# A two-layer encoder on one core: the gate's rows through DRAM and a broadcast load in place of TensorE transposes

## The chip, the core and the metric

The kernel runs on one core of one Trainium2 chip. The metric is device time in microseconds (us), the median of several executions. Engines are named as the profile names them: PE is TensorE (matrix products; PEld are its weight loads), DVE is VectorE, ACT is ScalarE, POOL is GpSimd, SP is SyncE, which here only issues DMAs. Each engine takes its instructions in the order in which they stand; a DMA that an engine issues stands in that engine's queue too.

## The reference, cut to what matters

Two layers, each a mixer and a gated convolutional FFN, on x of 512 tokens by 1024 channels in float32. Every one of the four sub-layers is wrapped in the same way:

```python
m = silu(c) @ w + b                       # c: 1 x 1024, w: 1024 x 3072
shift, scale, gate = split(m, 3)
h = x * (1.0 + scale) + shift
x = layer_norm(ALPHA * x + (1.0 + gate) * f(h), g, b)
```

So each sub-layer needs one row of 1024 gates, the same for all tokens. f is a spatial-gating and pooling mixer (sub-layer 0), a Conformer convolution module (2), and a conv-FFN of inner width 2816 (1 and 3).

## The kernel before, in words

Tokens are held as four tiles x_94 to x_97 of 128 tokens (partitions) by 1024 channels. A float32 product is made of three passes: each operand is split into a rounded part and the remainder (whi and wlo for weights, hhi and hlo for h, ahi and alo for activations), ACT casting the first, DVE subtracting for the second, and PE does high by high, high by low, low by high (`mm3`). Weights come in tiles of 128 by 1024 (512 KB) through SP's queue into four buffers w, and are split into seven buffers each of whi and wlo. PSUM has eight banks `ps`.

The modulations are dot products on DVE: rows of `in_ada` are loaded, multiplied with silu(c) on all partitions and summed, so that channel 128 c + p of a modulation stands in column c of partition p of `mods[i]` (128 by 24; the gate is columns 16 to 23). `gate_column` (line 199) makes the tile gcol, 128 by 8, of (1 + gate) / ALPHA. The accumulations `accumulate` (line 233) and `take` (line 378) multiply a PSUM tile, tokens on partitions, with the gate, so they want the row of 1024 gates on every partition: the tile gate, 128 by 1024, one buffer. `gate_bcast` (line 204) makes it: eight times it gives PE one column of gcol, repeated 128 times, as the weights, and the identity as the moving operand, which puts the column's 128 values into 128 columns of PSUM on all partitions; ACT copies the two filled banks into gate.

This happens four times: `gate_bcast(g0)` in the mixer of layer 0 (line 729, its column made at line 636), in each `ffn` at tile i = 10 (line 466), and in the Conformer module at tile i = 4 (line 919).

The order of the work is fixed in two ways. In the mixer of layer 0 (`in_order`, `pool_order` on) every instruction keeps the place in which it is written. Elsewhere only pinned ones do; the tile framework's scheduler, which plans with a model of the times, places the others. So an edit also moves instructions that it doesn't name. In the FFN of layer 0 (`ffn` with `side0`, `ahead0`) DVE does the dot products of three modulations beside the convolutions, POOL builds diagonal matrices whi and wlo from the identity and the taps (`diagonal`), and SP's queue holds weight loads, loads of in_ada, and stores (keephi, keeplo) of those diagonals and of split weights for layer 1, all in one line. `to_next` (line 395) ends a sub-layer: for each token tile it finishes the output product, takes the statistics on DVE (`take`), centres x (`centre`), transposes x on PE and makes the next h.

Of the kernel before, what the change touches and what calls it, by code (L numbers as in the profile page):

```python
# [7 lines left out]
F32 = mybir.dt.float32  # L8
# [4 lines left out]
P = 128  # L13
D = 1024
# [76 lines left out]
def body(ctx, tc, a):  # L91
# [8 lines left out]
    def psum():  # L100
        return pp.tile([P, 512], F32, name="ps")

    def tmp(n=512, dtype=F32):
        return tp.tile([P, TW], dtype, name="t")[:, 0:n]
# [4 lines left out]
    T, V, A, Q = (_Engine(e, pin, in_order) for e in (nc.tensor, nc.vector, nc.scalar, nc.sync))  # L109
    G = _Engine(nc.gpsimd, pin, pool_order)  # L110

    def behind(ins, other):

        if other is not None:
            tc.add_manual_dep(ins.ins, other.ins.name, ORDER, reason="issue order")
        return ins
# [13 lines left out]
    ident = const.tile([P, P], F32, name="ident")  # L130
# [4 lines left out]
    def col(name, i, n=1):  # L135
        at, _ = _COLS[name]
        return cols[:, at + i : at + i + n]


    def load(src):  # L140
        w = wp.tile([P, 1024], F32, name="w", bufs=4)
        Q.dma_start(w, src)
        return w
# [4 lines left out]
    def parts(w, after=None, eng=None, low_after=None, at=slice(0, 1024)):  # L148
        hi = wp.tile([P, 1024], F32R, name="whi", bufs=7)[:, at]
        lo = wp.tile([P, 1024], F32R, name="wlo", bufs=7)[:, at]  # L150
        w = w[:, at]
        if eng is None:
            behind(A.copy(hi, w), after)
        else:
            eng.tensor_copy(hi, w)
        behind(V.tensor_tensor(lo, w, hi.bitcast(F32), ALU.subtract), low_after)
        return hi, lo
# [5 lines left out]
    dp = ctx.enter_context(tc.tile_pool(name="dram", bufs=1, space=bass.MemoryType.DRAM))  # L163
# [32 lines left out]
    def ada_bias(i, j, n=1):  # L196
        V.tensor_tensor(mods[i][:, j : j + n], mods[i][:, j : j + n], col("ada_b", 24 * i + j, n), ALU.add)

    def gate_column(i):
        g = sm.tile([P, 8], F32, name="gcol")  # L200
        V.tensor_scalar(g, mods[i][:, 16:24], 1.0, 1.0 / ALPHA, ALU.add, ALU.mult)
        return g

    def gate_bcast(g):

        out = hp.tile([P, D], F32, name="gate", bufs=1)
        for h in range(2):
            ps = psum()
            for k in range(4):
                one = g[:, 4 * h + k : 4 * h + k + 1]  # L210
                T.transpose(ps[:, k * P : (k + 1) * P], one.broadcast_to([P, P]), ident)
            A.copy(out[:, h * 512 : (h + 1) * 512], ps)
        return out

    def affine(i, ln):
# [33 lines left out]
    def new_h():  # L249
        return (hp.tile([P, KD, S], F32R, name="hhi", bufs=1), hp.tile([P, KD, S], F32R, name="hlo", bufs=1))  # L250
# [61 lines left out]
    def split_act(ap_, t):  # L312
        return act_lo(act_hi(ap_, t))
# [12 lines left out]
    def out_half(acts, wsrc, d, gate, before=None, side=None):  # L326

        pss = [psum() for _ in range(ST)]
        nk = 2 * len(wsrc)
        for kp in range(nk // 2):  # L330
            w = ready(wsrc[kp])
            if side:
                side()
            for k in (2 * kp, 2 * kp + 1):
                if before:
                    before(k)
                for s in range(ST):
                    out_one(pss[s], acts, w, k, s, nk, before is not None)
        for s in range(ST):
            accumulate(s, d, pss[s], gate, G)  # L340
# [89 lines left out]
    def proj_tiles(h, srcs, after=None):  # L430

        out = []
        for s_ in srcs:
            w = tuple(v.rearrange("p (k m) -> p k m", k=KD) for v in ready(s_, after))
            ps = psum()
            for k in range(KD):
                mm3(ps, sl(w, slice(None), k), sl(h, slice(None), k), k == 0, k == KD - 1)
            out.append(ps)
        return out

    def conv3(l, f, ps):
        at = l * 132
        acc = tmp()
        A.activation(acc, ps, AF.Identity, bias=col("ffn_dw_b", l * 44 + f), scale=col("ffn_dw", at + 44 + f))
        V.scalar_tensor_tensor(acc[:, 1:S], ps[:, 0 : S - 1], col("ffn_dw", at + f), acc[:, 1:S], ALU.mult, ALU.add)
        V.scalar_tensor_tensor(acc[:, 0 : S - 1], ps[:, 1:S], col("ffn_dw", at + 88 + f), acc[:, 0 : S - 1], ALU.mult, ALU.add)
        return acc

    def ffn(ap_, l, h, ps4, last, mod_i, side, side_out=None):

        def pair(i, pg, pv):
            g = conv3(l, i, pg)
            v = conv3(l, NF + i, pv)
            gl = tmp()
            A.activation(gl, g, AF.Gelu_apprx_tanh)
            V.tensor_tensor(gl, gl, v, ALU.mult)
            return split_act(ap_, gl)

        w = a["ffn_up"]
        acts = []  # L460
        for i in range(NF):
            pg, pv = ps4[2 * i : 2 * i + 2] if i < 2 else proj_tiles(h, [w[l, 2 * i], w[l, 2 * i + 1]], last[0] if i < 5 else None)
            acts.append(pair(i, pg, pv))
            side(i)
            if i == 10:
                gate = gate_bcast(gate_column(mod_i))
            if i == SPLIT - 1:
                for d in range(2):
                    out_half(acts, [a["ffn_downA"][l, d, kp] for kp in range(SPLIT // 2)], d, gate, side=side_out)
                acts = []  # L470
        out_half(acts, [a["ffn_downB"][l, 0, kp] for kp in range((NF - SPLIT) // 2)], 0, gate, side=side_out)
        return acts, gate


    h = new_h()
    in_order.on = pool_order.on = True
    with tc.tile_pool(name="l0", bufs=1) as l0, tc.tile_pool(name="l0a", bufs=8) as ap_:
# [71 lines left out]
        def mod_dot(*js):  # L549
            for j in js:  # L550
                ada_dot(1, j, place(j))
# [50 lines left out]
        for hd in range(4):  # L602
            ps = psum()
# [5 lines left out]
        def sgu_gate(hd):  # L609
            ps, t = mixed[hd], us[hd]  # L610
            n_ = ps.rearrange("p (n q) -> p n q", n=ST)
            V.scalar_tensor_tensor(n_, n_, col("sgu_g", hd), bsb[:, hd : hd + 1, :].broadcast_to([P, ST, P]), ALU.mult, ALU.add)
            V.tensor_tensor(t, ps, t, ALU.mult)
            return act_hi(ap_, t)
# [12 lines left out]
        p = [sgu_gate(0), sgu_gate(1)]  # L627
# [4 lines left out]
        p = [sgu_gate(2), sgu_gate(3)]  # L632
        gate_dot(22, 23)
        fetch(x[1], a["x"][1])
        ada_bias(0, 16, 8)
        g0 = gate_column(0)
        mod_dot(0, 1)
        acts[2], acts[3] = (act_lo(q) for q in p)
        zr = []
# [77 lines left out]
        out0(5)  # L717
        acts[5], acts[4] = act_lo(p1), act_lo(p0)
        wl[2] = parts(wl[2])
        up = [load(a["ffn_up"][0, j]) for j in range(2)]  # L720
        mod_dot(14, 15)
        wl[3] = parts(wl[3])
# [3 lines left out]
        up[1] = parts(up[1])  # L726
        ada_bias(1, 0, 16)
        ga_be = affine(1, 0)
        gate = gate_bcast(g0)
        for s in range(ST):  # L730
            accumulate(s, 0, pss[s], gate, G)
        in_order.on = pool_order.on = False
        h, ps4, last = to_next(order, wl, gate, ga_be, [*up, a["ffn_up"][0, 2], a["ffn_up"][0, 3]])
# [36 lines left out]
    def side0(i):  # L770
        deferred(0, i)
        if i == 2:
            A.copy(taps_hi, taps)
            V.tensor_tensor(taps_lo, taps, taps_hi.bitcast(F32), ALU.subtract)
        if i >= 9 and todo_d:
            diagonal(*todo_d.pop(0))
        if i in (13, 15, 17):
            ahead0()
        for _ in range(3 if i >= 2 else 0):
            if todo:  # L780
                m, j = todo.pop(0)
                ada_tile(m, j, first)
                if j == 23:
                    ada_bias(m, *((16, 8) if m == 1 else (0, 24)))

    with tc.tile_pool(name="taps", bufs=1) as tp_, tc.tile_pool(name="f0", bufs=12) as ap_:
        taps_hi = tp_.tile([P, TAPS * KD], F32R, name="taphi")
        taps_lo = tp_.tile([P, TAPS * KD], F32R, name="taplo")
        acts, gate = ffn(ap_, 0, h, ps4, last, 1, side0, ahead0)
        h, ps4, last = to_next(acts, [a["ffn_downB"][0, 1, kp] for kp in range((NF - SPLIT) // 2)], gate, affine(2, 1), [a["cv_in"][j] for j in range(4)])  # L790


    with tc.tile_pool(name="l1", bufs=1) as l1, tc.tile_pool(name="l1a", bufs=25) as ap_:
# [119 lines left out]
        for i in range(KD):  # L913
            if i < 2:
                pa, pg = ps4[2 * i], ps4[2 * i + 1]
            else:
                pa, pg = proj_tiles(h, nxt)
                if i == 4:
                    gate = gate_bcast(gate_column(2))
                if i + 1 < KD:  # L920
                    nxt = [recall(("cv_in", j)) for j in (2 * i + 2, 2 * i + 3)]
                advance(now[0], V_TAPS)
            glu(i, pa, pg)
            if i:
                advance(now[1], G_TAPS)
            advance(todo_d, D_TAPS)
# [129 lines left out]
        h, ps4, last = to_next(acts, wo[1], gate, affine(3, 2), [a["ffn_up"][1, j] for j in range(4)], 2)  # L1056
# [9 lines left out]
    with tc.tile_pool(name="f1", bufs=12) as ap_:  # L1066
        acts, gate = ffn(ap_, 1, h, ps4, last, 3, side1)
# [105 lines left out]
```

## Time and profile before

| what | value |
|---|---|
| median of 3 runs | 1080.02 us (1079.01 to 1080.77) |
| the profiled execution | 1076.26 us |
| its span, first to last instruction | 1074.5 us |
| granted TensorE clock, mean over the span | 0.997 |
| PE busy | 1051.1 us, 98% of the span |
| DVE, ACT, POOL busy | 787.1, 462.2, 266.0 us |
| DMA | 214.23 MB, mean 199 GB/s |

The profiled execution is one run, 3.76 us below the median of the three timed ones; 1.76 us of it lie around the span. Of a row of a timeline the first number is the start in us from the span's start, the second what it took; a bracket at the end gives how long the engine was idle before it and what released it. Matmuls overlap in such rows (a matmul is shown with 0.39 us, and the next starts 0.23 us later), so PE's cost is read from starts.

### The profile page before, as it was taken

The numbers are of one execution on the slowest core, as the hardware profiler recorded it, in microseconds if no ns is written. First come the engines' busy times: TensorE is split into PE (matmuls) and PEld (weight loads), VectorE is DVE, ScalarE is ACT, GpSimd is POOL, SyncE is SP. The second block draws the span as 40 slices with busy tenths as digits, with TensorE's granted clock in tenths as the row PEclk, the third lists the DMA queues.
The fourth block names the chain that finished last, engine by engine and source line by source line (L and its number), as shares of the span: only waits on it lengthen the run. The fifth ranks groups of instructions, "written<-read, shape, count | busy, mean of one in ns | idle before, by whom it ended". The sixth has DMA issues, their size and how long they took to land.

```text
span 1074.5 us, 13947 instructions
## 1 busy us (share of the span) xinstructions
PE 1051.1 (98%) x5157; PEld 882.4 (82%) x5157; DVE 787.1 (73%) x1173; ACT 462.2 (43%) x676; POOL 266.0 (25%) x309
## 2 busy tenths in 40 slices
PE   6999999999999999999999999899999999999997
PEld 5888798888888887888988987798888888888886
DVE  6788879979966889956399999777676333656537
ACT  4544464433742444633666743564444212434300
POOL 0000200057026940001199995200000022000011
PEclk9999999999999999999999999999999999999999
DMA  9979418777998898971555471233332233323302
GB/s 353 408 264 369 169 42 280 268 266 258 384 413 333 335 331 306 337 294 59 222 210 191 157 260 50 99 121 116 117 118 85 92 98 99 98 98 99 98 1 78
DMA packets 61555, 214.23 MB, mean 199 GB/s; under 512 B 6960, under 2 KB 6960, under 8 KB 61488
## 3 DMA queue, kind: packets, MB, share of 16 engines
q1 hardware_dynamic: 59184, 209.16, 54.3%
q10 hardware_dynamic: 2304, 4.20, 1.6%
q8 instruction: 40, 0.66, 0.2%
q14 instruction: 27, 0.22, 0.1%
HBM read 182.13 MB, written 31.20 MB: 199 GB/s over the span
## 4 chain that ended last, share of the span: by engine, by line
PE 89%; DVE 5%; DMA 4%; POOL 2%; ACT 0%; issue 0%; SPq 0%; DVEq 0%; POOLq 0%
PE ps L85 89%; DMA w<-in_ffn_up 1%; DVE t L85 1%; DVE wlo L85 1%; DMA w<-in_cv_out 1%; POOL whi L85 1%; DMA w<-in_ab_in 1%; DVE ps L85 1%; DVE st L85 1%; DVE w L85 1%; ACT whi L85 0%; POOL wlo L85 0%; DMA whi<-keephi_cv_out 0%; POOL x L85 0%; DVE x L85 0%
## 5 line engine op out<-in xcount | busy, mean ns | idle before, releaser
L85 PE MATMUL ps<-hhi,whi 128*128 128x512 f32 (+1 forms) x960 | 353.1, 369 | 0.3 <-ACT whi L85 0.3
L85 PE MATMUL ps<-hhi,wlo 128*128 128x512 f32 (+1 forms) x960 | 352.8, 368 | 0.5 <-DVE wlo L85 0.5
L85 PE MATMUL ps<-hlo,whi 128*128 128x512 f32 (+1 forms) x960 | 352.9, 368 | 0.0
L85 DVE TENSOR_TENSOR wlo<-w,whi 128x1024 fp32r<-128x1024 f32 x176 | 219.1, 1253 | 167.1 <-ACT whi L85 163.8
L85 ACT CAST whi<-w 128x1024 fp32r<-128x1024 f32 x175 | 183.1, 1051 | 304.4 <-PE ps L85 180.6
L85 PEld LDWEIGHTS ps<-hhi,wlo 128*128 128x128 f32 x960 | 181.0, 188 | 31.1 <-DVE wlo L85 1.0
L85 PEld LDWEIGHTS ps<-hlo,whi 128*128 128x128 f32 x960 | 181.0, 189 | 29.8
L85 PEld LDWEIGHTS ps<-hhi,whi 128*128 128x128 f32 x960 | 180.5, 189 | 30.3 <-ACT whi L85 0.7
L85 POOL TENSOR_TENSOR x<-x,t 128x512 f32<-128x512 f32 x32 | 48.4, 1540 | 537.7 <-DVE t L85 537.7
L85 PE MATMUL ps<-whi,ahi 128*128 128x512 f32 (+1 forms) x426 | 167.8, 394 | 0.0
L85 PE MATMUL ps<-whi,alo 128*128 128x512 f32 (+1 forms) x426 | 166.3, 390 | 0.0
L85 PE MATMUL ps<-wlo,ahi 128*128 128x512 f32 (+1 forms) x426 | 166.3, 390 | 0.0
L85 DVE SCALAR_TENSOR_TENSOR t<-ps,cols,t 128x511 f32<-128x511 f32 x176 | 130.2, 745 | 5.9 <-ACT t L85 4.3
L85 POOL TENSOR_TENSOR a<-a 128x512 f32<-128x512 f32 (+1 forms) x99 | 104.7, 1094 | 23.6 <-ACT a L85 23.1
L85 ACT ACTIVATE t<-ps,cols 128x512 f32<-128x512 f32 (+1 forms) x108 | 78.1, 740 | 42.7 <-PE ps L85 41.2
L85 PEld LDWEIGHTS ps<-wlo,ahi 128*128 128x128 f32 x426 | 80.2, 188 | 18.7 <-issue 0.5
L85 PEld LDWEIGHTS ps<-whi,ahi 128*128 128x128 f32 x426 | 80.1, 188 | 18.6 <-issue 0.5
L85 PEld LDWEIGHTS ps<-whi,alo 128*128 128x128 f32 x426 | 80.1, 188 | 18.5
L85 DVE CUSTOM_DVE_ANT_0 w<-w,cb 128x1024 f32<-128x1024 f32 x56 | 69.6, 1251 | 9.2 <-DMA w<-in_ada 9.1
L85 ACT ACTIVATE a<-a,cols 128x512 f32<-128x512 f32 (+1 forms) x105 | 62.9, 634 | 26.5 <-POOL a L85 25.4
L85 DVE SCALAR_TENSOR_TENSOR ps<-a,cols,ps 128x512 f32<-128x512 f32 (+1 forms) x122 | 72.2, 661 | 0.0
L85 POOL TENSOR_SCALAR whi<-ident,taphi 128x128 fp32r<-128x128 f32 x62 | 47.3, 781 | 85.0 <-DMA w<-in_ffn_up 75.1
(105 smaller groups left out, 980.6 us busy)
## 6 DMA issues: line engine op xcount, KB each, us to landing
w<-in_ffn_up SPq DMA_DIRECT2D x88, 512.0 KB, 4.2
w<-in_ada SPq DMA_DIRECT2D x56, 512.0 KB, 4.6
x<-in_ada SPq DMA_DIRECT2D x24, 512.0 KB, 7.7
w<-in_ffn_downA SPq DMA_DIRECT2D x24, 512.0 KB, 4.2
w<-in_ffn_downB SPq DMA_DIRECT2D x20, 512.0 KB, 4.4
w<-in_cv_in SPq DMA_DIRECT2D x16, 512.0 KB, 6.9
keephi_cv_in<-whi SPq DMA_DIRECT2D x12, 512.0 KB, 6.3
keeplo_cv_in<-wlo SPq DMA_DIRECT2D x12, 512.0 KB, 6.3
```

What stands on the lines that cost most here:

```text
L85: ins = getattr(self.engine, name)(*args, **kw)
```

## The change

The transposes, their two PSUM banks and ACT's two copies go. In their place each gate column is written to a DRAM row of 1024 floats as soon as it is made, by a DMA that POOL issues: element by element, 128 partitions by 8 values of 4 bytes. The tile gate is then filled by one DMA on SP's queue that reads the row for all 128 partitions (512 KB moved). In the mixer of layer 0 the load is written into SP's line ahead of the loads of the FFN's first weights; elsewhere the scheduler sets its place.

```diff
-    def gate_bcast(g):
+    gate_rows = {}
+
+    def gate_out(i):
+
+        gate_rows[i] = dp.tile([1, D], F32, name=f"gate{i}")
+        G.dma_start(gate_rows[i].rearrange("o (c p) -> p (o c)", p=P), gate_column(i))
+
+    def gate_bcast(i):
 
         out = hp.tile([P, D], F32, name="gate", bufs=1)
-        for h in range(2):
-            ps = psum()
-            for k in range(4):
-                one = g[:, 4 * h + k : 4 * h + k + 1]
-                T.transpose(ps[:, k * P : (k + 1) * P], one.broadcast_to([P, P]), ident)
-            A.copy(out[:, h * 512 : (h + 1) * 512], ps)
+        Q.dma_start(out, gate_rows[i].partition_broadcast(P))
         return out
...
             if i == 10:
-                gate = gate_bcast(gate_column(mod_i))
+                gate = gate_bcast(mod_i)
...
         ada_bias(0, 16, 8)
-        g0 = gate_column(0)
+        gate_out(0)
...
         wl[2] = parts(wl[2])
+        gate = gate_bcast(0)
         up = [load(a["ffn_up"][0, j]) for j in range(2)]
...
         ga_be = affine(1, 0)
-        gate = gate_bcast(g0)
...
                 if j == 23:
                     ada_bias(m, *((16, 8) if m == 1 else (0, 24)))
+                    gate_out(m)
...
                 if i == 4:
-                    gate = gate_bcast(gate_column(2))
+                    gate = gate_bcast(2)
```

The scheduler moves other instructions with it. Three places of the lines follow, before and of the change (in names, a number such as 94 in x_94 is a buffer's own; ISA is DVE's dot product).

First, DVE at the end of the mixer of layer 0, from the accumulations with the gate (t<-ps,gate) to the first token tile's statistics. Before:

```order
L85 TENSOR_TENSOR t<-ps,gate 128x512 x4
L85 BN_STATS st<-x_94 128x6
L85 TENSOR_TENSOR wlo<-w,whi 128x1024
L85 BN_STATS st<-x_95 128x6
L85 BN_STATS st<-x_96 128x6
L85 BN_STATS st<-x_97 128x6
L85 TENSOR_TENSOR t<-ps,gate 128x512
L85 TENSOR_TENSOR x_94<-x_94,t 128x512
L85 BN_STATS st<-x_94 128x6
L85 BN_AGGR mv<-st 128x2
```

Of the change:

```order
L85 TENSOR_TENSOR t<-ps,gate 128x512 x4
L85 TENSOR_TENSOR wlo<-w,whi 128x1024
L85 BN_STATS st<-x_94 128x6
L85 BN_STATS st<-x_95 128x6
L85 TENSOR_TENSOR t<-ps,gate 128x512
L85 BN_STATS st<-x_96 128x6
L85 TENSOR_TENSOR x_94<-x_94,t 128x512
L85 BN_STATS st<-x_97 128x6
L85 BN_STATS st<-x_94 128x6
L85 BN_AGGR mv<-st 128x2
```

The weight's remainder wlo now stands ahead of all four first statistics, so one more of them lies between it and the first tile's BN_AGGR.

Second, DVE in the FFN of layer 0 at the middle of its down-projection, where the third gate column is made. Before:

```order
L85 TENSOR_SCALAR ga<-mod_92 128x8
L85 TENSOR_SCALAR gcol<-mod_92 128x8
L85 TENSOR_TENSOR be<-ga,cols 128x8
L85 TENSOR_TENSOR be<-be,mod_92 128x8
L85 TENSOR_TENSOR ga<-ga,cols 128x8
L85 TENSOR_TENSOR wlo<-w,whi 128x1024
L85 TENSOR_TENSOR t<-ps,gate 128x512 x4
L85 TENSOR_TENSOR wlo<-w,whi 128x1024 x2
```

Of the change:

```order
L85 TENSOR_SCALAR gcol<-mod_92 128x8
L85 TENSOR_SCALAR ga<-mod_92 128x8
L85 TENSOR_TENSOR t<-ps,gate 128x512
L85 TENSOR_TENSOR be<-ga,cols 128x8
L85 TENSOR_TENSOR t<-ps,gate 128x512
L85 TENSOR_TENSOR be<-be,mod_92 128x8
L85 TENSOR_TENSOR ga<-ga,cols 128x8
L85 TENSOR_TENSOR wlo<-w,whi 128x1024
L85 TENSOR_TENSOR t<-ps,gate 128x512 x2
L85 TENSOR_TENSOR wlo<-w,whi 128x1024 x2
```

The first wlo, of the weights that PE multiplies with next, has gone behind two of the accumulations. On POOL the write of the row stands at the same place, ahead of the adds x<-x,t that these accumulations feed, and the diagonal that stood there goes behind two of the adds:

```order
L85 DMA gate_3119<-gcol 128x8x1
L85 TENSOR_TENSOR x_94<-x_94,t 128x512
L85 TENSOR_TENSOR x_95<-x_95,t 128x512
L85 TENSOR_SCALAR whi<-ident,taphi 128x128 x8
L85 TENSOR_TENSOR x_96<-x_96,t 128x512
L85 TENSOR_TENSOR x_97<-x_97,t 128x512
L85 TENSOR_SCALAR wlo<-ident,taplo 128x128 x8
```

Before, five of those whi and no DMA stood ahead of the add to x_94.

Third, SP's line later in the same FFN, where two weight loads for PE stand beside the store of a split weight for layer 1 (the numbers are tiles'). Before:

```order
L85 DMA w<-in_ada 128x1024 x3
L85 DMA keephi_cv_out_1_3673<-whi 128x1024
L85 DMA keeplo_cv_out_1_3674<-wlo 128x1024
L85 DMA w<-in_ffn_up 128x1024 x2
L85 DMA w<-in_ada 128x1024 x3
```

Of the change:

```order
L85 DMA w<-in_ada 128x1024 x3
L85 DMA keephi_cv_out_1_3659<-whi 128x1024
L85 DMA w<-in_ffn_up 128x1024
L85 DMA keeplo_cv_out_1_3660<-wlo 128x1024
L85 DMA w<-in_ffn_up 128x1024
L85 DMA w<-in_ada 128x1024 x3
```

The first weight load no longer stands behind the store that waits for DVE's wlo.

## Rows read from the trace of the kernel before

**Rows 1.** The page, parts 1 (busy time) and 4 (chain that ended last).
```profile
PE 1051.1 (98%) x5157; PEld 882.4 (82%) x5157; DVE 787.1 (73%) x1173; ACT 462.2 (43%) x676; POOL 266.0 (25%) x309
...
PE 89%; DVE 5%; DMA 4%; POOL 2%; ACT 0%; issue 0%; SPq 0%; DVEq 0%; POOLq 0%
```

**Rows 2.** Waits of PE: waiter, releaser: us in total, times, longest us.
```profile
PE ps L85 <- DVE wlo L85: 1.0, 2, 0.5
...
PE ps L85 <- DVE x L85: 0.4, 1, 0.4
PE ps L85 <- ACT whi L85: 0.3, 1, 0.3
```

**Rows 3.** Instructions on tile gcol (ns min/median/max); timeline of PE, second gate.
```profile
L85 PE MATMUL ps<-ident,gcol x32: 270/272/273, 116.8 to 823.0; 128*128 128x128 f32 x32
L85 DVE TENSOR_SCALAR gcol<-mod x4: 165/166/172, 83.9 to 439.8; 128x8 f32<-128x8 f32 x4
...
265.07 0.39 PE L85 MATMUL ps<-hhi,wlo 128*128 128x512 f32 x1
265.30 1.03 PE L85 MATMUL ps<-ident,gcol 128*128 128x128 f32 x8
...
266.40 0.40 PE L85 MATMUL ps<-hlo,whi 128*128 128x512 f32 x1
```

**Rows 4.** Timeline of PE, first gate.
```profile
116.58 0.39 PE L85 MATMUL ps<-whi,alo 128*128 128x512 f32 x1
...
117.92 0.40 PE L85 MATMUL ps<-wlo,ahi 128*128 128x512 f32 x1
```

**Rows 5.** Timeline, end of the mixer of layer 0.
```profile
124.59 2.05 DVE L85 TENSOR_TENSOR wlo<-w,whi 128x1024 fp32r<-128x1024 f32 x1 [0.52 <-ACT whi L85]
126.56 1.96 DVE L85 BATCH_NORM_STATS2 st<-x 128x6 f32<-128x512 f32 x3
...
132.32 1.11 PE L85 MATMUL ps<-ident,x 128*128 128x128 f32 x8 [0.42 <-DVE x L85]
```

**Rows 6.** Timeline, middle of the down-projection, FFN of layer 0: DVE, then PE.
```profile
337.83 0.17 DVE L85 TENSOR_SCALAR gcol<-mod 128x8 f32<-128x8 f32 x1
...
339.23 1.23 DVE L85 TENSOR_TENSOR wlo<-w,whi 128x1024 fp32r<-128x1024 f32 x1 [0.82 <-ACT whi L85]
342.40 2.79 DVE L85 TENSOR_TENSOR t<-ps,gate 128x512 f32<-128x512 f32 x4 [1.95 <-PE ps L85]
...
344.76 0.39 PE L85 MATMUL ps<-hhi,wlo 128*128 128x512 f32 x1
```

**Rows 7.** Timeline of POOL, same stretch and after; instructions on tile ident.
```profile
343.18 1.30 POOL L85 TENSOR_TENSOR x<-x,t 128x512 f32<-128x512 f32 x1 [1.44 <-DVE t L85]
...
384.57 3.42 POOL L85 TENSOR_SCALAR wlo<-ident,taplo 128x128 fp32r<-128x128 f32 x7
...
L85 POOL TENSOR_SCALAR whi<-ident,taphi x62: 365/372/2467, 221.8 to 384.2; 128x128 fp32r<-128x128 f32 x62
```

**Rows 8.** The chain that ended last, in order of time, late in that FFN.
```profile
401.29 1.24 DVE wlo L85
...
402.54 0.33 SPq L85
...
402.92 6.00 DMA w<-in_ffn_up
...
408.94 1.06 ACT whi L85
```

**Rows 9.** DMA issues (count, KB, us to landing); timeline of SP.
```profile
cb<-in_c SPq DMA_DIRECT2D x1, 512.0 KB, 4.8
...
cols<-in_cols SPq DMA_DIRECT2D x1, 48.0 KB, 4.6
...
103.71 15.20 SPq L85 DMA_DIRECT2D w<-in_ffn_up  x6
```

**Rows 10.** Windows: busy us of PE, PEld, DVE, ACT, POOL (instructions); Conformer module.
```profile
580.00:600.00 20.00, 20.00 (x90) 16.57 (x89) 18.57 (x28) 12.46 (x19) 19.92 (x20) 1.00 0.49 171
```

## The prediction

> **What bounds the kernel now.** I read the page first: PE is busy for 1051 of 1074.5 us, and the chain that ended last runs 89% through PE [rows 1]. So whatever PE no longer issues is worth its full time, unless another engine then makes PE wait. The second view is therefore PE's waits, to see who stands close behind: DVE's centred x once for 0.4 us, a weight's whi once for 0.3, its wlo twice for 1.0 [rows 2]. These are short, but each marks a place at which PE and another chain arrive together, and where time that is taken from PE alone comes back as a wait. The third view is the timeline around the four places of the change, on PE [rows 3, 4] and on its neighbours [rows 5 to 7]. About 0.2% of the time, 2.2 us, is what a measurement of this kernel can tell from no change.
>
> **What goes.** Each transpose is shown with 272 ns [rows 3], but they overlap, and eight are over in about 1 us. What they cost is read from starts. At the second gate the last ordinary matmul starts at 265.07, and the second one behind the transposes at 266.40: 1.33 us [rows 3]. Without transposes these two starts are two paces apart, 2 x 0.23 (265.07 to 265.30 is one pace [rows 3]), so the eight cost 1.33 - 0.46 = 0.87 us. At the first gate 116.58 to 117.92 gives 1.34 - 0.46 = 0.88 [rows 4]. In all four places PE goes from matmul to transposes and back without a wait, so I count 4 x 0.87 = 3.5 us of PE's line. ACT's two copies per gate I cost at nothing: ACT is busy 43% of the span [rows 1], and what covers them (PE's own work) stays.
>
> **What comes.** Four column writes on POOL's queue, four row loads on SP's queue.
>
> The load moves 512 KB to 128 partitions from one row, as the load of c does, which landed in 4.8 us [rows 9]. I cost it at nothing. The first is issued around 103.7, where SP starts on six weight loads that need 15 us because they wait for buffers [rows 9]; the loads behind it are the cover, and they wait for buffers anyway. In SP's line each row load stands where its column is long written (the column of the first is made at 83.9 [rows 3]), so SP isn't held by it.
>
> The write has no counterpart in this trace. For its issue on POOL the nearest row is SP's issue of a DMA of 128 rows, 0.33 us [rows 8]; that is the lower end. It has 1024 pieces of 4 bytes, eight times as many, so 8 x 0.33 = 2.6 us is the next end. POOL's instructions are also stretched by what runs beside them: the same diagonal took between 365 and 2467 ns [rows 7], a factor of 6.8, so 18 us is the far end. I take 2.6, since most of those diagonals (median 372 ns) were not stretched. For the time until the row has landed, the 48 KB of columns took 4.6 us in 128 pieces [rows 9]: from 4.6 to 8 x 4.6 = 37 us.
>
> At three places no POOL work stands near the write (POOL is busy 25% of the span [rows 1]). The third stands in a busy stretch: its column is made at 338.0, and POOL's next instruction of the change, the add to x_94, could start at 343.18 [rows 6, 7]. That leaves 5.2 us, and 2.6 fits. By the Trainium skill (DMA: Bandwidth & Descriptors, section Rules for kernel authors) a last dimension that isn't contiguous becomes one descriptor per element and should be rearranged, which speaks against this write. No run here shows yet what that costs. By the page's count the sum stays the same, since my 2.6 us are already the price of every element by itself.
>
> **What is moved.** Three places decide how much of the 3.5 us stays.
>
> First gate. PE's wait for the first centred x, 0.42 us, ends a DVE chain that begins with a weight's whi, for which ACT needs a buffer that PE frees, then wlo, then the statistics [rows 5]. PE comes 0.87 us earlier, so the chain can begin 0.87 earlier; but one statistic more now stands in it, 1.96 / 3 = 0.65 us [rows 5]. It ends 0.2 us earlier, or up to 0.9 if wlo, which took 2.05 us beside POOL's adds and takes 1.23 elsewhere [rows 5, 6], is no longer stretched. I take 0.4, so 0.5 of the 0.9 us come back as a wait.
>
> Middle of the down-projection. DVE's order puts wlo of PE's next weights behind two accumulations. From PE's release at 342.40 there are now t (2.79 / 4 = 0.70), a column operation (0.17), t, two more columns and wlo (1.23): 0.70 + 0.17 + 0.70 + 0.34 + 1.23 = 3.1 us, to 345.5. PE wants this wlo at 344.76 [rows 6]. A new wait of up to 0.8 us; starts overlap a little on DVE, so 0.4 is the lower end. I take +0.6.
>
> Late in that FFN. The chain runs from wlo over SP's store to the weight load and ACT's cast [rows 8], and PE waits there 0.3 and 0.5 us [rows 2]. With the load ahead of the store it starts about 1.3 us earlier (401.29 to 402.54 [rows 8]). That could remove 0.8; against it PE arrives earlier, and POOL's diagonals, which now start behind two adds, hold stores in the same line. I take -0.3, between -0.8 and +0.8.
>
> The Conformer module I take as passing its 0.87 on, and the last gate too.
>
> **The sum.** -3.5 + 0.5 + 0.6 - 0.3 = -2.7 us. Against the profiled execution's own 1076.26 us (span 1074.5 and 1.76 around it) that is 1073.6. The median of the runs is 3.76 higher; moved by the same amount it is 1080.02 - 2.7 = **1077.3 us**. The bounds: -3.5 - 0.8 + 0.4 = -3.9 with nothing given back at the first gate and the best of the other places, -3.5 + 0.7 + 0.8 + 0.8 = -1.2 with the worst.
>
> **The rivals.**
>
> *The gain is given back where others stand close behind.* Besides the three places, DVE and POOL in the Conformer module are nearly as full as PE: 18.6 and 19.9 of 20 us [rows 10]. If its 0.87 is lost there on top of the upper bound, -1.2 + 0.9 = -0.3 us: 1079.7, and 1078.8 at the bound itself. For it: each wait of rows 2 is a tie. Against it: the last two of the four gates stand where PE shows no wait near them. No change within 0.2%: chance 0.28.
>
> *POOL is held by the third write, and SP's line behind POOL.* Ends slower. The write's issue on POOL is stretched beyond the 5.2 us that it has. POOL then builds diagonals without a pause to 388 (384.57 + 3.42 [rows 7]), SP's stores wait for them, two weight loads stand behind each store, and the wait at the end of that stretch says there is no slack left. Each us over 5.2 goes through. At 12 us of issue: +6.8 - 2.7 = +4.1, 1084.1. It decides slower from 5.2 + 2.7 + 2.2 = 10 us. For it: the factor 6.8 of rows 7. Against it: it needs a stretch of nearly 4 on top of the eightfold price, and DVE is idle for 2 us just then [rows 6]. The Trainium skill (SBUF — State Buffer, section SBUF: two separate sides) has such a mechanism: a DMA issued from POOL has its descriptors written by GpSimd, which DVE can lock out of a port they share. The diagonals' stretch agrees with a lock of that kind. Chance 0.10.
>
> *The first row lands late.* Written at 84.1, wanted by SP at 103.7: 19.6 us. At the far end of 37 us SP stands 17 us, and with it six weight loads [rows 9]; their wlo stands ahead of the accumulations on DVE, so PE would wait for most of that. Slower from some 25 us on; at 30 us +10 - 2.7, 1087. For it: pieces of 4 bytes. Against it: the pieces of the 48 KB transfer are shared among many engines, and eightfold is the worst scaling. Chance 0.04.
>
> **How the numbers follow.** My forecast, the transposes' time comes off PE and about a fifth of it returns, has 0.58; it includes a gain of up to 5 us if waits at ties vanish. Faster by over 0.2%: 0.57 (the forecast without its last corner). Within: 0.29. Slower: 0.14. The range goes from 1074.8 (the lower bound -3.9, and 1.3 us for the run's own scatter of about 0.9 us each way and a tie that opens) to 1081.0, over all of the second case and the start of the third; about 0.09 lie above it and as much below. The likeliest case's own range is 1075 to 1078.
>
> **What would show it.** Right: 32 matmuls fewer on PE, busy time down by some 3.5 us; at the first gate a wait of about 0.9 us for x instead of 0.4; a new short wait for wlo near 341; waits late in that FFN below 0.8; the four loads landing in about 5 us; POOL's issue under 5 us. Wrong: PE's waits sum up to 3 us more than before (second case), or SP or POOL idle behind the row's DMA with PE waiting for a weight.

## The result and the profile after

| | median of 6 runs | lowest to highest |
|---|---|---|
| before | 1080.24 us | 1079.01 to 1085.41 |
| after | 1091.71 us | 1086.02 to 1097.80 |

The ratio is 1.0111, 95% interval 1.0085 to 1.0137: the change makes the kernel 11.5 us slower, where 1077.3 was forecast and 1081.0 was the end of the range. The profiled execution of after took 1092.78 us with a span of 1091.0, 16.5 more than that of before; its mean granted clock is 0.987, before 0.997.

The page of after, parts 1, 3 (the new queue) and 4, against [rows 1]:

```profile
PE 1056.9 (97%) x5125; PEld 885.0 (81%) x5125; DVE 783.6 (72%) x1173; ACT 458.2 (42%) x668; POOL 270.3 (25%) x313
...
q0 software_dynamic: 128, 0.02, 0.0%
...
PE 64%; DMA 15%; DVE 11%; issue 6%; ACT 1%; POOL 1%; SPq 1%; DVEq 0%; ACTq 0%; POOLq 0%
```

PE has 32 matmuls fewer, as it should, yet is busy 5.8 us longer. The chain now spends 15% of the span in DMAs, before 4%. The new queue carries 0.02 MB, 0.0% of the engines' time: by this row alone it would be dismissed.

The waits of PE in after (waiter, releaser: us in total, times, longest), against [rows 2]:

```profile
PE ps L85 <- DVE x L85: 5.0, 1, 5.0
PE ps L85 <- DVE t L85: 4.3, 4, 1.9
PE ps L85 <- ACT whi L85: 3.3, 1, 3.3
PE ps L85 <- DMA whi<-keephi_cv_out: 3.1, 1, 3.1
```

The 0.4 us for the centred x has become 5.0, and the waits for t were 1.6 us in two before; the last row stood there before, too, with the same 3.1. All gaps between PE's matmuls together are 19.8 us, before 8.9. Around the longest, the windows of after (busy us of PE, PEld, DVE, ACT, POOL with their counts, granted clock, DMA share, GB/s) show what follows such a wait:

```profile
132.00:136.00 4.00, 0.23 (x2) 0.00 (x0) 3.82 (x8) 0.00 (x0) 1.66 (x2) 0.80 0.42 131
136.00:140.00 4.00, 2.77 (x11) 2.58 (x12) 3.23 (x7) 1.58 (x5) 0.56 (x1) 0.50 0.00 0
140.00:144.00 4.00, 4.00 (x16) 3.16 (x15) 2.41 (x5) 2.56 (x6) 0.55 (x1) 0.84 0.02 4
144.00:148.00 4.00, 4.00 (x23) 3.37 (x22) 2.70 (x6) 3.03 (x8) 0.55 (x1) 1.00 0.00 0
```

PE stood from 132.23 to 137.23, and the granted clock fell to 0.50, the lower of its two levels (1.2 GHz), until about 141. PE counts as busy there, with 11 and 16 instructions for 23 in the last window. That is why its busy time rose. Over the span the missing clock is 1091.0 x 0.013 = 14 us against 1074.5 x 0.003 = 3, so about 11 us of clock are missing more than before; 10.9 us more are waits, and the transposes give 3.5 back. The sum, 18.4, is 1.9 above the 16.5 that the span grew: the ends of the waits at 132 and 398 us lie in slow stretches already and are counted in both. Not every wait brings the lower clock: before, PE stood 3.1 us at 674 us, and the windows from 672 to 684 us have 1.00. Nor is all of the missing clock the writes' doing: two of the slow stretches of after, 3.4 us each at 684 and 694 us, stand also in unread_32B below, which lost nothing.

Where do the waits come from? The chain of after that ends in this wait, followed from 84 us on:

```profile
85.48 16.09 DMA vn<-in_ada
...
101.64 10.98 DMA hlo<-in_ada
...
112.68 10.13 DMA w<-in_ffn_up
...
122.88 1.06 ACT whi L85
...
133.60 0.67 DVE x L85
```

Three loads one behind the other, each issued as the one ahead has landed, take 37 us. Before, the chain of this stretch held no load: from 84 us on it was 39.5 us of PE's own work, then ACT's whi. The DMA view of 84 to 102 us in after (count, KB each, median us to landing), with the write itself in its last row:

```profile
hlo<-in_ada SPq DMA_DIRECT2D x7, 512.0 KB, 12.0
vn<-in_ada SPq DMA_DIRECT2D x2, 512.0 KB, 16.1
w<-in_ab_out SPq DMA_DIRECT2D x2, 512.0 KB, 16.8
x<-in_x SPq DMA_DIRECT2D x1, 512.0 KB, 17.1
gate<-gcol POOLq DMA_DIRECT2D x1, 4.0 KB, 14.5
```

The same loads before, in the same window:

```profile
hlo<-in_ada SPq DMA_DIRECT2D x6, 512.0 KB, 6.1
vn<-in_ada SPq DMA_DIRECT2D x3, 512.0 KB, 7.1
w<-in_ab_out SPq DMA_DIRECT2D x3, 512.0 KB, 7.9
x<-in_x SPq DMA_DIRECT2D x1, 512.0 KB, 8.0
```

What the engines moved meanwhile stands in the windows of after:

```profile
88.00:92.00 4.00, 4.00 (x34) 3.83 (x33) 4.00 (x5) 0.58 (x1) 0.00 (x0) 1.00 1.29 266
92.00:96.00 4.00, 4.00 (x22) 3.22 (x21) 2.66 (x6) 0.59 (x1) 0.00 (x0) 1.00 1.12 56
96.00:100.00 4.00, 4.00 (x16) 2.78 (x15) 0.66 (x1) 2.52 (x4) 0.00 (x0) 1.00 0.89 136
100.00:104.00 4.00, 4.00 (x38) 3.96 (x36) 2.98 (x6) 0.00 (x0) 0.00 (x0) 1.00 0.89 328
```

From 92 to 96 us the 16 DMA engines are booked as busy without a pause (share 1.12) and move 56 GB/s, against 328 a little later and 412 before in the same window. Their single packets tell the same: a 4096-byte packet of SP's queue usually takes 0.16 us; beside this write they took up to 6.04 us, beside the second 4.60, beside the third, where the engines are booked with 0.35 and less from 356 to 364 us, 2.34, beside the fourth 7.37. A DMA share near 1 says that packets are open on the engines, not that they move anything. The write's own packets are booked with almost nothing, 1.4 us together, and the last of them ends at 92.9 us; the loads stay slow up to about 100, when the write lands (84.6 + 14.5). So the trace shows who is held up, and when, but not inside of what.

At the second gate there is one thing more, on SP's queue in after:

```profile
195.34 0.33 SPq L85 DMA_DIRECT2D w<-in_ada  x1
205.46 0.33 SPq L85 DMA_DIRECT2D gate<-gate  x1
```

SP stands for 9.8 us at the row load, which waits for the write, and the loads behind it stand too; from 200 to 204 us the DMA engines move 30 GB/s.

So there were three theories. **The pieces:** the 1024 pieces of 4 bytes hold up the DMA engines, weight loads beside them land late, PE waits, and its clock falls. **SP:** the row load's wait holds SP's line. **The order:** the scheduler's new order, or the row loads, cost the time, and the writes are harmless.

### The profile page after: what moved, and what is told of

It reads as the page before. It is cut to its first block, busy times and chain, and to the rows that moved or that the text cites. A ratio compares the mean times of both kernels' runs of the same rounds, so it can differ in the third digit from the quotient of the medians.

```text
span 1091.0 us, 13876 instructions
## 1 busy us (share of the span) xinstructions
PE 1056.9 (97%) x5125; PEld 885.0 (81%) x5125; DVE 783.6 (72%) x1173; ACT 458.2 (42%) x668; POOL 270.3 (25%) x313
## 4 chain that ended last, share of the span: by engine, by line
PE 64%; DMA 15%; DVE 11%; issue 6%; ACT 1%; POOL 1%; SPq 1%; DVEq 0%; ACTq 0%; POOLq 0%
PE ps L85 64%; DMA w<-in_ffn_up 4%; DMA w<-in_cv_in 4%; DVE wlo L85 2%; DVE t L85 2%; DMA vn<-in_ada 2%; DVE x L85 2%; DMA w<-in_cv_out 2%; DVE a L85 1%; DVE w L85 1%; ACT whi L85 1%; DVE ps L85 1%; DMA hlo<-in_ada 1%; DMA gate<-gcol 1%; DMA w<-in_ab_in 1%
## 5 line engine op out<-in xcount | busy, mean ns | idle before, releaser
L85 ACT CAST ahi<-t 128x512 fp32r<-128x512 f32 x52 | 32.2, 619 | 76.0 <-DVE t L85 75.8
```

Of the source, the lines that this page charges most:

```text
L85: ins = getattr(self.engine, name)(*args, **kw)
```

## Experiments

In all short diffs, G is POOL, A is ACT, Q is SP, V is DVE, T is PE.

### The write away, the write alone

no_write:

```diff
-        G.dma_start(gate_rows[i].rearrange("o (c p) -> p (o c)", p=P), gate_column(i))
+        gate_column(i)
...
-        Q.dma_start(out, gate_rows[i].partition_broadcast(P))
+        Q.dma_start(out, a["c"].partition_broadcast(P))
```

> The changed kernel without its four writes; the row loads stay in their places and read the row of c, which is there from the start, so the gate is c's row and not the computed one. Theory: about 1077 us (before less the 3.5 us of transposes and some of it given back), no wait over 1 us of TensorE at 132 and 284. Rival B (the order, or the row loads themselves, which move 0.5 MB each): 1086 to 1094. The order is not wholly the same, since nothing waits for a write now.

Measured: 1081.2 us, ratio 1.0018 (1.0002 to 1.0034). So 10.5 of the 11.5 us are gone with the writes. Expected was about 1077 with no wait over 1 us at 132: PE waits 1.5 us there, and the time is 4 us longer. DVE's and SP's orders differ from those of after as well, so that this run alone doesn't settle it.

before_plus_write: the kernel before, with gate_column followed by the POOL write, which nothing reads; the columns are made where the change makes them.

```diff
+        G.dma_start(gate_rows[i].rearrange("o (c p) -> p (o c)", p=P), g)
```

> The kernel before (transposes kept, gate from TensorE) with the four writes of 4-byte pieces added, which nobody reads. Theory: slower than before by what the pieces do to other loads, 1083 to 1092 us, with loads of 4 KB a partition at 84 to 102 us landing in 12 us or more, and a wait of TensorE near 132 us. Rival B, and the rival that only the wait of SP for the write counts: 1079 to 1081 us.

Measured: 1091.29 us, ratio 1.0117 (1.0090 to 1.0143). Four writes that nobody reads, 4 KB each, cost the kernel before as much as the whole change. PE has the order of before, and on DVE 13 of 1173 instructions stand elsewhere, on ACT 6, on SP 4. Neither the new order nor SP's wait can be the cause of this. The place was partly missed: its PE waits 2.5 us at 112 for alo and 3.3 at 271 for t, and only 0.4 near 136.

### The pieces with and without the wait for them

write_unread:

```diff
-        Q.dma_start(out, gate_rows[i].partition_broadcast(P))
+        Q.dma_start(out, a["c"].partition_broadcast(P))
```

> The changed kernel with its four writes of 4-byte pieces, but the row loads read the row of c and so wait for no write; the gate is c's row. It parts the two halves of the theory. If the slow DMA engines are the larger half: the wait near 132 us stays at 3 to 5 us with the half clock behind it, 1083 to 1090 us. If SP standing before the second row load is the larger half: the wait near 132 us stays and those near 284 to 287 us and later go; 1080 to 1084. If neither: 1089 to 1094.

Measured: 1093.08 us, ratio 1.0121 (1.0089 to 1.0152), no better than after. SP no longer stands for the second write, and the time is the same, so the loss doesn't need **SP**. That SP's wait has some part in after itself isn't excluded: 189 of DVE's instructions and 33 of SP's stand elsewhere than in after. The time lies above the 1083 to 1090 that I had for the first theory, in the range that I had kept for neither of the two (1089 to 1094): the wait near 284 to 289 us, which I had put down to SP, came back larger. PE's waits in write_unread:

```profile
PE ps L85 <- DVE t L85: 5.3, 3, 3.8
PE ps L85 <- DVE x L85: 5.0, 1, 5.0
```

unread_32B, the deciding run: the same with the row in the order (p c), so that the 8 values of a partition lie side by side.

```diff
-        G.dma_start(gate_rows[i].rearrange("o (c p) -> p (o c)", p=P), gate_column(i))
+        G.dma_start(gate_rows[i].rearrange("o (p c) -> p (o c)", p=P), gate_column(i))
```

> As write_unread (the row loads read the row of c; the gate is c's row), with the writes in 128 pieces of 32 bytes instead of 1024 of 4, still issued by POOL. The instructions stand as in write_unread on TensorE, VectorE, ScalarE and SP; only the size of the pieces differs, and no multiply reads with a stride. Theory (the 4-byte pieces hold the DMA engines): 1080 to 1083 us, as no_write (1081.2), no packet of 4096 B over 2 us at 90 to 100 us, the wait near 132 us down to 1.5 us. Rival A (any write through POOL's queue holds them): 1090 or more, as write_unread (1093.1).

Measured: 1077.3 us, ratio 0.9976 (0.9961 to 0.9991), 2.7 us under the range, which I had taken from no_write. All engines, POOL too, have the same instructions in the same order as in write_unread, and gcol is read alike; only on the DRAM side are the pieces eight times as large and an eighth as many. That takes 15.8 us off. Whether their number, their size or the spread of their addresses counts (neighbouring values of a partition lie 512 bytes apart in the one, side by side in the other) no run tells apart. Windows of write_unread, and then of unread_32B:

```profile
92.00:96.00 4.00, 4.00 (x29) 3.68 (x29) 4.00 (x6) 1.18 (x2) 0.00 (x0) 1.00 1.24 82
...
200.00:204.00 4.00, 4.00 (x19) 3.31 (x18) 1.23 (x1) 0.03 (x1) 0.00 (x0) 1.00 1.02 69
...
288.00:292.00 4.00, 1.31 (x4) 0.49 (x2) 4.00 (x6) 3.13 (x5) 0.00 (x0) 0.50 1.00 297
```

```profile
92.00:96.00 4.00, 4.00 (x16) 2.59 (x15) 3.38 (x6) 0.91 (x2) 0.00 (x0) 1.00 1.03 410
...
200.00:204.00 4.00, 4.00 (x19) 3.31 (x18) 4.00 (x7) 3.76 (x5) 0.00 (x0) 1.00 0.64 206
...
288.00:292.00 4.00, 4.00 (x19) 3.23 (x18) 4.00 (x5) 2.52 (x4) 0.00 (x0) 1.00 1.02 417
```

In unread_32B the engines move 410 GB/s beside the first write, no 4096-byte packet at 90 to 100 us takes over 1 us, and DVE is full at 200 us, where in write_unread it works 1.23 us of 4 for want of data. That gap at 200 comes out on PE 90 us later, at 288, as a wait with half clock: followed back from there, the chain of write_unread is mostly DVE at work, with two loads of 6 and 7 us between, and it reaches back to a load of in_ada that was issued at 197.8 us, beside the write, and took 14.0. PE's wait for x is 1.5 us, for 5.0 in write_unread. The write's own issue is cheap in both, and its landing isn't what is waited for. Instructions on tile gate, write_unread and then unread_32B (ns min/median/max):

```profile
L85 POOL DMA_DIRECT2D gate<-gcol x4: 922/936/1077, 86.1 to 459.2; - x4
```

```profile
L85 POOL DMA_DIRECT2D gate<-gcol x4: 582/589/744, 83.1 to 440.1; - x4
```

### Which queue, which write

act_queue: write_unread with `A.dma_start` in place of `G.dma_start`.

> As write_unread, with the writes of 4-byte pieces issued by ScalarE's queue instead of POOL's. Theory (the pieces, not the queue): the loads beside them are held as before, 1089 to 1095 us. Rival A (POOL's software queue is what is slow): 1080 to 1084 us. The row of c is the gate here too, and a few instructions stand in another order.

Measured: 1089.61 us, ratio 1.0077 (1.0049 to 1.0105). The pieces slow the loads from ScalarE's queue as well (45 GB/s at 196 to 200 us; a write took up to 19.0 us to land). It is 3.5 us better than POOL's queue, in an order that differs a little; the intervals overlap, and I don't separate the two. Where the 4-byte pieces are issued from is not the cause. On ScalarE's queue the trace books the pieces one by one: 1040 packets of 4 bytes for a write, 9 ns each as a rule, 2.9% of the engines' time from 84 to 104 us for the first write. On POOL's queue it books 16 packets of 256 bytes and 16 of 4, whatever the size of the pieces, so that view doesn't show them.

first_4B and late_4B: unread_32B with the 4-byte order for one write, or for the last two.

```diff
+        way = "o (c p) -> p (o c)" if i == 0 else "o (p c) -> p (o c)"
```

> As unread_32B (1077.3 us), but the first write, at 84 us, goes in 4-byte pieces again; the three others keep 32 bytes, and the order of instructions is that of write_unread and unread_32B on every engine. Theory that the loss lies in the first two writes, which fall where the loads are late for TensorE: the first write's part is the wait near 132 us (4.99 us against 1.49) and half of the 6.83 us at half clock behind it, 3.5 + 3.4 = 6.9 us, so 1084 us (1082 to 1086). Rival, that each write costs the same, a quarter of 15.8 us: 1081.2 us.

Measured: 1082.81 us, ratio 1.0034 (1.0020 to 1.0048): the first write costs 5.5 us by the medians (6.3 by the ratios), with PE's wait for x at 4.4 us. That is in the range of the first theory and above the equal share.

> The same with the third and fourth writes, at about 355 and 460 us, in 4-byte pieces and the first two in 32 bytes. Theory: the loads beside them are held up too, but TensorE has work enough in hand, 1077 to 1080 us. Rival, that each write costs the same: 1077.3 + 7.9 = 1085.2 us.

Measured: 1078.07 us, ratio 0.9989 (0.9975 to 1.0002): the last two cost 0.8 us, which these intervals don't tell from nothing. Windows of late_4B, beside the fourth write:

```profile
444.00:448.00 4.00, 4.00 (x19) 3.33 (x18) 2.60 (x5) 0.00 (x0) 0.00 (x0) 1.00 1.16 206
448.00:452.00 4.00, 4.00 (x20) 3.30 (x19) 0.00 (x0) 0.00 (x0) 0.00 (x0) 1.00 1.03 102
452.00:456.00 4.00, 4.00 (x19) 3.32 (x18) 0.80 (x1) 1.89 (x3) 0.00 (x0) 1.00 0.85 160
```

The same kind of stall, 102 GB/s where unread_32B moves 382 in the same window: DVE and ACT stand for over 4 us, and PE is full throughout; its next wait over 0.2 us comes at 627 us, in unread_32B at 625. So PE has work enough in hand here, and I read the price of a stall as set by that; the run shows it for these two writes only. The second write's price, 15.8 - 5.5 - 0.8 = 9.5 us (8.0 by the ratios), is by difference only.

### What the removal alone brings

no_gate_dma: neither write nor load; the gate is the tile cb.

```diff
-        out = hp.tile([P, D], F32, name="gate", bufs=1)
-        Q.dma_start(out, gate_rows[i].partition_broadcast(P))
-        return out
+        return cb
```

> No transposes, no write and no row load: the gate is the tile that holds silu of c on all partitions from the start. It says what taking the transposes away brings by itself, and what the four row loads cost. If the four row loads and their place in SP's queue took the gain: 1076 to 1078 us. If the saved 3.5 us are given back anyway where TensorE waits for VectorE, ScalarE and loads (about 131, 391 to 411, 668 to 677 us): 1079.5 to 1082, like no_write.

Measured: 1077.96 us, ratio 0.9971 (0.9954 to 0.9988), 2 to 3 us under before. That is the range that I had for row loads which take the gain, but the row loads and the unread 32-byte writes add nothing visible: unread_32B has both and took 1077.3. no_write, with less to do, took 1081.2; its gaps on PE sum to 15.1 us against 10.8 in unread_32B, the largest new one 2.3 us for a whi at 411 us. The two differ in the scheduler's order. I count 4 us as what an order alone can do here, and read no smaller difference between kernels of different orders.

### Three ways that compute the gate

w_contig: the 32-byte write, read back, with the order (p c) undone by each multiply.

```diff
-            V.tensor_tensor(t, ps, gate[:, cs], ALU.mult)
+            V.tensor_tensor(t.rearrange("q (c p) -> q c p", p=P), ps.rearrange("q (c p) -> q c p", p=P), gate[:, d * 4 : d * 4 + 4], ALU.mult)
```

> The changed kernel with one thing different: the gate is kept in DRAM in the order (partition, column), so that each write is 128 pieces of 32 bytes in place of 1024 pieces of 4 bytes; the multiply by the gate reads it with a stride. Instructions stand in the same order on every engine as in the changed kernel. Theory (the pieces of 4 bytes hold up the DMA engines, so that weight loads land late and SP stands before the second row load): about 1077 us, 1075 to 1081, the waits at 132 and 284 to 287 us gone or under 0.5 us, the write landing in under 5 us. Rival A (the write's queue and route through POOL are slow whatever the size of the pieces): the write still lands in 10 us or more, SP still stands before the second row load, 1086 to 1092. Rival B (the new order of the instructions is the loss): 1089 to 1094 with the waits where they were.

Measured: 1086.41 us, ratio 1.0071 (1.0048 to 1.0095): 5.3 us better than after in the same order of PE, DVE, POOL and SP, but not the 1077 that I expected. It is a time of rival A, whose condition fails: no packet at 90 to 100 us takes over 1 us, and the writes land in 3.8 to 5.9 us, where that rival wants 10 or more. SP still stands 2.6 us before the second row load. What is new is the multiply, from instructions on tile gate:

```profile
L85 DVE TENSOR_TENSOR t<-ps,gate x49: 589/1180/1254, 122.4 to 1080.3; 128x512 f32<-128x512 f32 x47, 128x256 f32<-128x256 f32 x2
```

Reading the gate with a stride of 32 bytes makes it 1180 ns (691 before). I had changed two things at once.

copy_order: w_contig's write and load, into a weight buffer; one ScalarE copy puts the row in order.

```diff
+        row = load(gate_rows[i].partition_broadcast(P))
+        A.copy(out.rearrange("q (c p) -> q c p", p=P), row.rearrange("q (p c) -> q c p", c=KD))
```

> The gate computed in full: w_contig's 128 pieces of 32 bytes, but the row lands in a weight buffer and one ScalarE copy a gate puts it into channel order, so that the 49 multiplies by the gate read without a stride again (691 ns and not 1180). Theory, that w_contig's 9 us over unread_32B are its strided multiplies, 49 x 0.49 us = 24 us of VectorE: 1077 to 1081 us. Rival, that it was SP's wait for the write: 1084 to 1088 us. A weight buffer is taken for each gate, which may cost a few us.

Measured: 1081.81 us, ratio 1.0009 (0.9989 to 1.0029), between the ranges of the theory and the rival. With a copy in place of the strided multiplies 4.6 of w_contig's 9 us are gone, little more than the 4 that an order can do, and the orders differ. The copy takes 2.19 us (a cast of the same size 1.05), and PE waits 3.4 us once for a whi. Copy, weight buffer and order aren't told apart in the rest.

write_row: the column is first transposed once on PE, so that the write is 8 pieces of 512 bytes.

```diff
+        ps = psum()[0:KD, 0:P]
+        T.transpose(ps, gate_column(i), ident)
+        row = tmp(P)[0:KD]
+        A.copy(row, ps)
+        G.dma_start(gate_rows[i].rearrange("o (c p) -> (o c) p", p=P), row)
```

> The gate computed as in the changed kernel, by way of DRAM, but its column is first transposed once by TensorE to 8 rows of 128 and copied by ScalarE, so that the write is 8 pieces of 512 bytes; the load and the multiply are those of the changed kernel. Theory: 1079 to 1083 us, like no_write (four transposes of 8 by 128 add 0.1 to 0.4 us each), with no packets held up. Rival A: 1088 or more. If the 32-byte run's 1086.4 was owed to its strided multiply (1180 ns against 691), this one comes out 4 us or so under it.

Measured: 1086.4 us, ratio 1.0063 (1.0038 to 1.0088). Expected 1079 to 1083: missed, for another reason than the rival's. The timeline of PE in write_row:

```profile
77.34 0.39 PE L85 MATMUL ps<-whi,hlo 128*128 128x512 f32 x1
84.35 0.37 PE L85 MATMUL ps<-ident,gcol 128*8 128x128 f32 x1 [6.62 <-DVE gcol L85]
84.37 0.78 PE L85 MATMUL ps<-whi,hhi 128*128 128x512 f32 x1
```

PE takes its instructions in order, and I had put the transpose 6.6 us ahead of the column it needs. Matmuls behind it are shown with up to 0.78 us for 0.39; the windows from 80 to 88 us have a clock of 0.51 and 0.50.

row_later: the same, the first transpose behind the window means.

```diff
-        gate_out(0)
+        g0 = gate_column(0)
...
         m3, m2 = pool_mean(3), pool_mean(2)
+        gate_out(0, g0)
```

> The gate computed in full: write_row with one difference, the transpose of the first gate's column to 8 rows of 128 stands 66 rows later in TensorE's order, after the window means, so that TensorE doesn't stand 6.62 us at 77.7 us for the column. Theory: write_row lost 6.6 us of idle time there and half of the 10.24 us at half clock behind it, so it comes from 1086.4 to about 1076 to 1080 us, and would be as fast as the kernel before or faster by up to 0.3%. Rival, that a row load which waits for its write costs time in SP's order also where the pieces are large: 1083 to 1087 us.

Measured: 1079.04 us, ratio 1.0001 (0.9989 to 1.0013). 7.4 us come back with the place of one transpose and of the copy and write that hang on it. PE's waits in row_later:

```profile
PE ps L85 <- DMA whi<-keephi_cv_out: 3.7, 1, 3.7
PE ps L85 <- DVE a L85: 2.3, 2, 1.4
PE ps L85 <- ACT whi L85: 2.0, 2, 1.7
PE ps L85 <- DVE wlo L85: 1.7, 3, 0.7
PE ps L85 <- DVE t L85: 1.5, 2, 1.2
PE ps L85 <- DVE x L85: 1.5, 1, 1.5
```

The wait for x is 1.5, not 5.0. With pieces of 512 bytes, the change as meant (the gate by way of DRAM) is neither faster nor slower than before. No version that computes the gate beat it.

## Why the prediction was wrong

**The step that failed** is in "What comes": the write was priced only by its own issue and landing, and both were taken as covered. Its effect on other transfers has no term in the sum. The issue is 0.93 us (taken: 2.6, bounds 0.33 and 18), the landing 11.0 to 15.2 us (bounds 4.6 and 37), so the terms that I had were within bounds and harmless. The missing term is 10.5 us by no_write, 11.1 by before_plus_write, and 15.8 between write_unread and unread_32B, the last two in nearly the same and in the same order.

**The argument that hid it** stands in the third rival: "the pieces of the 48 KB transfer are shared among many engines, and eightfold is the worst scaling". That asks how soon the write itself is done, and by that it was no worse than the bounds; what it does to the loads on the same engines isn't asked. The rival's price was for a late row; what came late was everything beside it. Its chance of 0.04 was set on the wrong consequence.

**By the page's count the sum stays the same** was the sentence on the Trainium skill (DMA: Bandwidth & Descriptors, section Rules for kernel authors), whose rule spoke against this write. This case agrees with the rule: the step from 1024 pieces to 128 is worth 15.8 us. I had charged its descriptors to POOL alone. In unread_32B POOL's issue is only 0.35 us shorter, so that was the wrong account. The lock between DVE and POOL's descriptors (the Trainium skill, SBUF — State Buffer, section SBUF: two separate sides) can't be the main thing, since act_queue loses 9.6 us with no write on POOL.

**"SP isn't held by it"** was wrong: SP stood 9.8 us at the second row load, issued 11 us behind its write. A cost of it doesn't show (after 1091.71, write_unread without it 1093.08), as far as two different orders can tell. The POOL rival's condition didn't come: the third issue took 0.94 us, not over 5.2. At its place, the end of that stretch, PE does wait 3.3 us in after (at 398), and the chain behind this wait runs through POOL's diagonals, SP's line and a load of 11.2 us beside the third write. write_unread has the same write and no wait there but 0.9 and 0.8 us at 427, so what those 3.3 us are owed to stays open.

**What the runs don't contradict:** the price of the 32 transposes. no_gate_dma gains 2.1 us by its medians (1080.03 to 1077.96), 3.1 by the ratio, where the sum had -2.7. But its order differs from that of before, and by my own count an order can do 4 us: the gain agrees with the term and doesn't show it. That unread_32B took the 1077.3 us that were forecast is luck; it doesn't read its row back, and its ties came out otherwise than in the sum. The first gate gives back more than the 0.5: PE waits 1.5 us for x in unread_32B, no_write and row_later, 0.4 before (0.5 in no_gate_dma). The new wait near 341 doesn't appear, in after or in unread_32B. Late in the FFN, where I had a gain of 0.3, PE waits for a whi 3.3 us in after, 2.3 in no_write and 1.7 in no_gate_dma; in unread_32B the two waits there are 0.9 us together, before 0.8.

**PE's clock** had no term either. I priced each wait at its length. Behind the waits of 5.0, 1.9 and 3.3 us in after (at 132, 284 and 398 us) the granted clock went to half for 3 to 7 us each; first_4B's 5.5 us are 2.9 us of longer wait (4.4 against 1.5), and the rest agrees with the 6.8 us at half clock that begin before the wait ends.

## What to carry to other kernels

Price a DMA by its pieces as well as its bytes, and charge them to every transfer in flight at that time: 4 KB in 1024 pieces of 4 bytes held up loads of 512 KB for 6 to 9 us, and in 128 pieces of 32 bytes nothing could be seen. What such a stall costs depends on the place: the last two writes cost 0.8 us, with PE full beside the fourth, and the first 5.5, where the slowed loads, one behind the other, became the chain that PE waited for. Where a transpose on PE brings a column into rows, place it behind the column in PE's order; 6.6 us of standing cost 7.4.

## What the runs showed of the hardware that was not expected

- Sixteen DMA engines at a share of 1.12 moved 56 GB/s; 4096-byte packets of another queue took up to 7.37 us for 0.16, while the 4-byte packets themselves were booked with 9 ns as a rule.
- The stall doesn't depend on POOL's software queue: issued by ScalarE, writes landed in up to 19.0 us, and 45 GB/s were moved beside one.
- A multiply on VectorE that reads one operand from SBUF with a stride of 32 bytes took 1180 ns for 691 (its three operands were written as 4 by 128 patterns, too); a ScalarE copy with such a stride 2.19 us, a cast of the same 128 by 1024 1.05.
- The transpose of one column to 8 rows is shown on PE with 0.27 us, but a wait of 6.62 us ahead of it brought about 10 us at the lower clock.
